# Feed-forward input products in a seven-product form, and modulation products in 512-wide pieces

## The chip, the cores and the metric

One core of a Trainium2 chip runs the whole program. The metric is device time in microseconds, the median of a few executions.

## The reference, cut to what matters

A two-layer backbone works on 640 tokens (128 context tokens, 512 latent ones) of width 1024, in float32. Each layer is a feed-forward half step, a mixer, and a second feed-forward half step:

```python
def swiglu(h, w_in, w_out):
    a, b = jnp.split(h @ w_in, 2, axis=-1)      # w_in: 1024 x 5632
    return (jax.nn.silu(a) * b) @ w_out         # w_out: 2816 x 1024

def ffn_half_step(x, mods, g, w_in, w_out):
    shift, scale, gate = mods
    return x + 0.5 * gate * swiglu(rmsnorm(x, g) * (1.0 + scale) + shift, w_in, w_out)
```

The mixers are a pooling and short-convolution mixer in layer 0 and an attention mixer in layer 1. Each layer has nine modulation vectors per condition (one condition for the context, one for the latent tokens): `silu(cond) @ mod_w + mod_b`, of which `mod_w` is 1024 x 9216 for each layer.

## The kernel before

**Layout.** Activations lie transposed: 128 features on the partitions, tokens along the free axis. The 640 tokens are two halves of 320 (`HALVES`). A matrix product in float32 is made of three products of rounded parts: each operand is split into a rounded part (`hi`, type fp32r) and the rest (`lo`), and `mm3` (lines 110 to 115) issues hi·hi, hi·lo and lo·hi. `split_w` (lines 95 to 101) makes the parts of a weight tile of 128 x 1024: ScalarE writes `whi`, VectorE subtracts and writes `wlo`; each has five buffers.

**A feed-forward stage** (`ffn`, four of them) goes over 22 pairs `j`: a 128-wide column block of the gate side and the matching one of the value side. `load_pair` loads two weight tiles of 512 KB and splits them. `pair_half` multiplies both by the normalised activations `h_hi`, `h_lo` of one token half (8 blocks of the contraction, three matmuls each), and `pair_tail` makes silu of the one times the other and splits the result into `ghi`, `glo`. So a pair is 2 sides x 2 halves x 8 blocks x 3 = 96 matmuls of 320 columns. After 4, 8, 12 and 17 pairs a group of pairs is complete; `out_group` multiplies it by its w_out tiles one pair later (8 output blocks x 2 halves x group size x 3 matmuls: 192 for a group of four) and `add_x` adds each block to `x` with the gate, in one VectorE instruction for the second half and two for the first. The last group goes through `out_last`, which computes the norm sums and the next stage's `h` on the way. Pairs 0 and 1 are done together, from weights that were fetched in the stage before; `me.second()` writes the second half of `h` while the first half multiplies.

**Modulation.** `gemv(l, m, q)` is one quarter of one modulation vector: two 512 KB loads (`mraw`, two buffers of its own), then on VectorE, for each of two conditions, one `tensor_scalar` and seven `scalar_tensor_tensor` of 256 columns, a transpose and a reduction of 512 columns. `todo` is the list of quarters; `step()` takes one after each pair and `drain()` takes what is left at the stage's end. The four feed-forward stages are given 6, 4, 5 and 1 vectors.

**Order of the work.** Engines run their instructions in order. The order is written by a scheduler at compile time: each instruction has the priority of its place in the program text, and on each engine the earliest instruction that the scheduler's own timeline holds to be ready goes next. The buffers of one tag are handed out to the instructions in the same way. TensorE's instructions follow the text almost exactly; VectorE's and ScalarE's may run ahead of it as far as buffers allow. All loads are issued from SyncE's queue.

## Time and profile before

| | |
|---|---|
| time, median of 3 runs | 2528.28 us |
| the three runs | 2528.28, 2528.24, 2536.61 us |
| span of the profiled execution | 2535.1 us |
| TensorE busy | 2485.0 us, 98% |
| VectorE busy | 1604.7 us, 63% |
| ScalarE busy | 731.5 us, 29% |
| granted TensorE clock, mean | 0.987 |

The profile is of one execution, from its first to its last instruction. Its own time is not listed apart from the three; the span fits the third, 2536.61 us, which leaves 1.5 us around it. Busy time of TensorE counts pipelined matmuls, so it says that matmuls followed each other, not how fast.

### The profile page before, as it was taken

The numbers are of one execution on the slowest core, as the hardware profiler recorded it, in microseconds if no ns is written. First come the engines' busy times: TensorE is split into PE (matmuls) and PEld (weight loads), VectorE is DVE, ScalarE is ACT, GpSimd is POOL, SyncE is SP. The second block draws the span as 40 slices with busy tenths as digits, with TensorE's granted clock in tenths as the row PEclk, the third lists the DMA queues.
The fourth block names the chain that finished last, engine by engine and source line by source line (L and its number), as shares of the span: only waits on it lengthen the run. The fifth ranks groups of instructions, "written<-read, shape, count | busy, mean of one in ns | idle before, by whom it ended". The sixth has DMA issues, their size and how long they took to land.

```text
span 2535.1 us, 40930 instructions
## 1 busy us (share of the span) xinstructions
PE 2485.0 (98%) x16594; PEld 2417.9 (95%) x16594; DVE 1604.7 (63%) x3520; ACT 731.5 (29%) x1339; POOL 155.5 (6%) x156
## 2 busy tenths in 40 slices
PE   6999999999999999999999999999999999999998
PEld 3999999999999999999999999999988799999998
DVE  6999993376599974337999933444447787333334
ACT  3322221243242222223222221344334442221222
POOL 2000000031110000002000000211001110000001
PEclk8999999999999999999999999999999899999999
DMA  7444442232144432222544412122111023222221
GB/s 262 134 159 149 167 142 75 67 94 82 59 134 150 165 118 84 72 70 84 167 158 151 150 67 76 67 86 80 49 64 36 17 93 116 75 75 75 75 76 42
DMA packets 81691, 257.44 MB, mean 102 GB/s; under 512 B 12896, under 2 KB 18656, under 8 KB 81504
## 3 DMA queue, kind: packets, MB, share of 16 engines
q1 hardware_dynamic: 81504, 254.84, 30.3%
q8 instruction: 130, 2.13, 0.4%
q14 instruction: 57, 0.47, 0.1%
HBM read 251.13 MB, written 3.67 MB: 101 GB/s over the span
## 4 chain that ended last, share of the span: by engine, by line
PE 94%; DVE 4%; DMA 1%; ACT 1%; issue 0%; SPq 0%; DVEq 0%; ACTq 0%
PE mm L113 25%; PE mm L114 25%; PE mm L115 25%; PE atb L723 2%; PE mmb L113 2%; PE mmb L114 2%; PE mmb L115 2%; PE sd L789 1%; PE m L114 1%; PE m L113 1%; PE m L115 1%; PE atb L717 1%; PE mmb L622 1%; PE mmb L623 1%; PE mmb L624 1%; PE sn L743 1%
## 5 line engine op out<-in xcount | busy, mean ns | idle before, releaser
L114 PE MATMUL mm<-h_lo,whi 128*128 128x320 f32 x2944 | 906.0, 308 | 1.7 <-DVE h_lo L233 1.7
L115 PE MATMUL mm<-h_hi,wlo 128*128 128x320 f32 x2944 | 906.5, 308 | 0.0
L113 PE MATMUL mm<-h_hi,whi 128*128 128x320 f32 x2944 | 901.1, 309 | 2.2 <-ACT h_hi L231 1.8
L99 ACT CAST whi<-raw 128x1024 fp32r<-128x1024 f32 x320 | 335.4, 1050 | 859.6 <-PE mm L114 762.6
L114 PEld LDWEIGHTS mm<-h_lo,whi 128*128 128x128 f32 x2944 | 553.0, 188 | 2.4 <-DVE h_lo L233 2.0
L113 PEld LDWEIGHTS mm<-h_hi,whi 128*128 128x128 f32 x2944 | 551.2, 188 | 3.6 <-ACT h_hi L231 2.0
L115 PEld LDWEIGHTS mm<-h_hi,wlo 128*128 128x128 f32 x2944 | 553.1, 188 | 0.0
L100 DVE TENSOR_TENSOR wlo<-raw,whi 128x1024 fp32r<-128x1024 f32 x302 | 371.9, 1232 | 215.5 <-ACT whi L99 214.6
L113 PE MATMUL mm<-ghi,whi 128*128 128x320 f32 x1408 | 436.4, 310 | 0.0
L115 PE MATMUL mm<-ghi,wlo 128*128 128x320 f32 x1408 | 435.8, 309 | 0.0
L114 PE MATMUL mm<-glo,whi 128*128 128x320 f32 x1408 | 435.4, 309 | 0.0
L143 DVE SCALAR_TENSOR_TENSOR gacc<-mraw,sc,gacc 128x256 f32<-128x256 f32 x896 | 383.5, 479 | 0.2
L239 DVE SCALAR_TENSOR_TENSOR x<-mm,gate,x 128x128 f32<-128x128 f32 (+2 forms) x480 | 195.2, 435 | 175.3 <-PE mm L115 174.5
L115 PEld LDWEIGHTS mm<-ghi,wlo 128*128 128x128 f32 x1408 | 264.7, 188 | 0.0
L113 PEld LDWEIGHTS mm<-ghi,whi 128*128 128x128 f32 x1408 | 264.7, 188 | 0.0
L114 PEld LDWEIGHTS mm<-glo,whi 128*128 128x128 f32 x1408 | 264.7, 188 | 0.0
L348 DVE TENSOR_TENSOR g<-silu,mm 128x320 f32<-128x320 f32 x168 | 81.8, 487 | 268.8 <-PE mm L115 267.2
L193 POOL TENSOR_TENSOR acc<-acc,sq 128x320 f32<-128x320 f32 x84 | 79.5, 946 | 1973.2 <-ACT sq L188 1966.1
L350 ACT CAST ghi<-g 128x320 fp32r<-128x320 f32 x176 | 80.4, 457 | 285.2 <-DVE g L348 284.9
L346 ACT ACTIVATE silu<-mm 128x320 f32<-128x320 f32 x168 | 72.8, 433 | 198.0 <-PE mm L115 197.8
L351 DVE TENSOR_TENSOR glo<-g,ghi 128x320 fp32r<-128x320 f32 x176 | 85.2, 484 | 21.6 <-ACT ghi L350 21.6
L188 ACT ACTIVATE sq<-x 128x320 f32<-128x320 f32 x98 | 45.6, 469 | 118.4 <-DVE x L239 91.2
(201 smaller groups left out, 2504.0 us busy)
## 6 DMA issues: line engine op xcount, KB each, us to landing
raw<-w_in SPq DMA_DIRECT2D x176, 512.0 KB
mraw<-mod_w SPq DMA_DIRECT2D x128, 512.0 KB
raw<-w_out SPq DMA_DIRECT2D x88, 512.0 KB
m<-mod_w SPq DMA_DIRECT2D x32, 256.0 KB
raw<-even_w SPq DMA_DIRECT2D x16, 512.0 KB
raw<-mix_w SPq DMA_DIRECT2D x16, 512.0 KB
raw<-odd_qk SPq DMA_DIRECT2D x16, 512.0 KB
raw<-odd_v SPq DMA_DIRECT2D x8, 512.0 KB
```

Of the source, the lines that this page charges most:

```text
L99: act.copy(hi, src)
L100: eng.tensor_tensor(lo, src, hi, ALU.subtract)
L113: pe.matmul(out, wh, xh, start=start, stop=False)
L114: pe.matmul(out, wh, xl, start=False, stop=False)
L115: pe.matmul(out, wl, xh, start=False, stop=stop)
L143: dve.scalar_tensor_tensor(out=acc[:, c, :], in0=w[k], scalar=sc[:, k, c:c + 1], in1=acc[:, c, :], op0=ALU.mult, op1=ALU.add)
L193: pool.tensor_tensor(acc, acc, s, ALU.add)
L239: dve.scalar_tensor_tensor(out=x[:, k, a:b], in0=ps[:, a - a0:b - a0], scalar=gate[:, c, k:k + 1], in1=x[:, k, a:b], op0=ALU.mult, op1=ALU ...
L346: act.activation(s, pa, AF.Silu)
L348: dve.tensor_tensor(g, s, pb, ALU.mult)
L350: act.copy(ghi[:, a:b], g)
L351: dve.tensor_tensor(glo[:, a:b], g, ghi[:, a:b], ALU.subtract)
```

## The change

**Seven products.** From pair 3 on (`NPLAIN = 3`) a pair is computed in Strassen's form. The 2 x 2 blocks are: halves of the tokens, halves of the contraction (blocks 0 to 3 and 4 to 7), and gate or value side. Seven products of four blocks each (7 x 4 x 3 = 84 matmuls) replace eight (96). `strassen_w` makes four sums of half weight tiles on VectorE and splits three whole tiles and one half tile where before two whole ones were split. Sums of `h` are made once per stage: `sums` after pairs 0 and 1, `sums7` after pair 2, into `q_hi`, `q_lo` and over the second half of `h_hi`, `h_lo`. For the next stages `h_chunk` writes the second half of an unsplit copy of `h` with one more ScalarE instruction per block. Partial results leave PSUM by four ScalarE copies and four VectorE sums per pair, and two accumulators are added to again after they were copied.

**Modulation.** A piece is now one 512 KB load and four VectorE instructions of 512 columns; four pieces make half a vector and end with two transposes and two reductions. The loads take their buffers from the weights' own ring (`raw`, five buffers where the weights had three). After pair 2 and each later pair `step` takes at least three pieces. One vector of layer 0 moves from the first feed-forward stage to the mixer behind it, so the stages now have 5, 1 (in the mixer), 4, 5 and 1 vectors, of eight pieces each.

**Buffers.** `ghi` and `glo` go from ten buffers to seven, the small tiles share one ring of eight.

```diff
+NPLAIN, GBUFS = 3, 7
...
-            w = wpool.tile([128, 1024], F32, tag="raw", bufs=3, name="raw")
+            w = wpool.tile([128, 1024], F32, tag="raw", bufs=5, name="raw")
...
+        def strassen_w(src_a, src_b):
+            ra, rb = load_w(src_a), load_w(src_b)
+            tt = scope[0].tile([128, 1024], F32, tag="tt", bufs=1, name="tt")
+            dve.tensor_tensor(tt[:, 512:1024], ra[:, 0:512], rb[:, 0:512], ALU.add)
+            x0 = split_w(ra)
+            dve.tensor_tensor(tt[:, 0:512], tt[:, 512:1024], rb[:, 512:1024], ALU.add)
+            dve.tensor_tensor(rb[:, 0:512], rb[:, 0:512], rb[:, 512:1024], ALU.add)
+            dve.tensor_tensor(ra[:, 0:512], tt[:, 0:512], ra[:, 512:1024], ALU.add)
+            x1 = split_w(tt)
+            x2 = split_w(rb)
+            hi = scope[0].tile([128, 512], F32R, tag="whi4", bufs=1, name="whi4")
+            lo = scope[0].tile([128, 512], F32R, tag="wlo4", bufs=1, name="wlo4")
+            act.copy(hi, ra[:, 0:512])
+            dve.tensor_tensor(lo, ra[:, 0:512], hi, ALU.subtract)
+            return [(t[0][:, o:o + 512], t[1][:, o:o + 512]) for t in (x0, x1, x2) for o in (0, 512)] + [(hi, lo)]
...
-        def gemv(l, m, q):
-            w = load_mod(A["mod_w"][l, m, q])
-            acc = scope[0].tile([128, 2, 256], F32, tag="gacc", bufs=1, name="gacc")
...
+        def gemv(l, m, q, i):
+            w = wpool.tile([128, 1024], F32, tag="raw", bufs=5, name="mraw")
+            sp.dma_start(out=w, in_=A["mod_w"][l, m, q, i])
+            if i == 0:
+                accs[0] = scope[0].tile([128, 2, 512], F32, tag="gacc", bufs=1, name="gacc")
+            acc = accs[0]
+            for j in range(2):
+                k, wk = 2 * i + j, w[:, j * 512:(j + 1) * 512]
                 for c in range(2):
...
+            for c in range(2):
+                at = scope[0].tile([128, 16, 32], F32, tag="gaccT", bufs=1, name="gaccT")
+                dve.transpose(at.rearrange("p b i -> p (b i)"), acc[:, c, :])
+                dve.tensor_reduce(part[:, c, 16 * q:16 * q + 16], at, axis=AX.X, op=ALU.add)
...
+        def step(n=2):
+            for _ in range(min(n, len(todo))):
+                gemv(*todo.popleft())
...
+                if whole is not None:
+                    act.activation(whole[:, a:b], t[:, a - a0:b - a0], AF.Identity, bias=sh[:, c, k:k + 1])
...
+                def sums(hs):
+                    n = NT if me.y is None else HT
+                    for k in range(8):
+                        dve.tensor_tensor(hs[k][:, 0:n], h_hi[:, k, 0:n], h_lo[:, k, 0:n], ALU.add)
+                    for k in range(4):
+                        (a11, a21), (a12, a22) = [(t[:, 0:HT], t[:, HT:NT]) for t in (hs[k], hs[k + 4])]
+                        dve.tensor_tensor(a22, a21, a22, ALU.subtract)
+                        dve.tensor_tensor(a21, a11, a21, ALU.subtract)
+                        dve.tensor_tensor(a11, a22, a11, ALU.subtract)
+                        dve.tensor_tensor(a12, a12, a11, ALU.add)
+                        for d, src in ((slice(0, 2), hs[k + 4].rearrange("p (a n) -> p a n", a=2)),
+                                       (slice(2, 3), a11.unsqueeze(1))):
+                            act.copy(q_hi[:, k, d, :], src)
+                            dve.tensor_tensor(q_lo[:, k, d, :], src, q_hi[:, k, d, :], ALU.subtract)
+
+                def sums7(hs):
+                    for k in range(4):
+                        act.copy(h_hi[:, k, HT:NT], hs[k][:, HT:NT])
+                        dve.tensor_tensor(h_lo[:, k, HT:NT], hs[k][:, HT:NT], h_hi[:, k, HT:NT], ALU.subtract)
...
+                def strassen_pair(j):
+                    b11, b21, t2, t1, t3, b22, t4 = strassen_w(w_in[2 * j], w_in[2 * j + 1])
+                    new_g(j)
+
+                    def prod(out, w, xs, first=True):
+                        for k in range(4):
+                            mm3(out, w, k, xs[k][0], xs[k][1], first and k == 0, k == 3, True)
+
+                    a, b = mmb([128, HT], "pa"), atb([128, HT], "pb")
+                    prod(a, b11, hs_op(0, 0))
+                    c11 = t320("t")
+                    act.copy(c11, a)
+                    prod(b, b21, hs_op(4, 0))
+                    dve.tensor_tensor(c11, b, c11, ALU.add)
+                    act.activation(c11, c11, AF.Silu)
+                    prod(a, t2, q_op(2), False)
+                    c12 = t320("t")
+                    act.copy(c12, a)
+                    ec = sb2("pe")
+                    e, c = ec[:, 0:HT], ec[:, 512:512 + HT]
+                    prod(e, t1, q_op(1))
+                    c22 = t320("t")
+                    act.copy(c22, e)
+                    prod(a, t3, hs_op(0, 1), False)
+                    c21 = t320("t")
+                    act.copy(c21, a)
+                    dve.tensor_tensor(c22, c22, a, ALU.subtract)
+                    prod(e, b22, q_op(0), False)
+                    dve.tensor_tensor(c12, e, c12, ALU.subtract)
+                    dve.tensor_tensor(c11, c11, c12, ALU.mult)
+                    g_split(j, c11, 0)
+                    prod(c, t4, hs_op(4, 1))
+                    dve.tensor_tensor(c21, c, c21, ALU.add)
+                    act.activation(c21, c21, AF.Silu)
+                    dve.tensor_tensor(c21, c21, c22, ALU.mult)
+                    g_split(j, c21, 1)
...
-                        step()
                         j = 2
...
+                    else:
+                        strassen_pair(j)
+                        j += 1
+                    if j == 2:
+                        sums(hs)
+                    if j == NPLAIN:
+                        sums7(hs)
+                    if j >= NPLAIN:
+                        step(max(3, -(-len(todo) // (NPAIR - j + 1))))
                     if pend is not None:
...
-                drain()
+                step(len(todo))
...
-            return [(l, m, q) for m in ms for q in range(4)]
+            return [(l, m, q, i) for m in ms for q in range(2) for i in range(4)]
...
-        todo.extend(pieces(0, 2, 3, 4, 5, 6, 7))
+        todo.extend(pieces(0, 2, 3, 4, 5, 6))
         ffn(0, FFN1, n_ffn[0][0], n_even, start)
+        todo.extend(pieces(0, 7))
         even_mixer(n_even, n_ffn[0][1])
```

## Rows read from the trace of the kernel before

**Rows 1.** The page: busy time of each engine, its share, instructions.

```profile
PE 2485.0 (98%) x16594; PEld 2417.9 (95%) x16594; DVE 1604.7 (63%) x3520; ACT 731.5 (29%) x1339; POOL 155.5 (6%) x156
```

**Rows 2.** The page: the chain that ended last, by engine.

```profile
PE 94%; DVE 4%; DMA 1%; ACT 1%; issue 0%; SPq 0%; DVEq 0%; ACTq 0%
```

**Rows 3.** Windows: four feed-forward stages, and a stretch inside the first.

```profile
core 0: us, PE busy (x) PEld busy (x) DVE busy (x) ACT busy (x) POOL busy (x), PEclk, DMA share, GB/s
...
200.00:400.00 200.00, 200.00 (x1367) 200.00 (x1366) 176.73 (x387) 45.54 (x68) 0.00 (x0) 1.00 0.45 147
...
72.00:540.00 468.00, 468.00 (x3203) 467.93 (x3204) 361.48 (x800) 120.89 (x196) 16.84 (x29) 1.00 0.39 128
710.00:1172.00 462.00, 460.19 (x3137) 459.93 (x3136) 297.97 (x634) 113.43 (x179) 9.37 (x10) 1.00 0.33 110
1195.00:1660.00 465.00, 464.94 (x3181) 464.60 (x3180) 332.33 (x716) 119.85 (x192) 16.77 (x16) 1.00 0.36 119
2053.00:2515.00 462.00, 462.00 (x3157) 462.00 (x3157) 209.47 (x406) 115.96 (x186) 8.74 (x10) 1.00 0.23 76
```

**Rows 4.** Groups by form, VectorE, 72 to 200 us: count, busy, mean, idle before.

```profile
L143 DVE SCALAR_TENSOR_TENSOR gacc<-mraw,sc,gacc 128x256 f32<-128x256 f32 x138 | 59.1, 477 | 0.1
L100 DVE TENSOR_TENSOR wlo<-raw,whi 128x1024 fp32r<-128x1024 f32 x20 | 24.3, 1216 | 1.6 <-ACT whi L99 1.5
L351 DVE TENSOR_TENSOR glo<-g,ghi 128x320 fp32r<-128x320 f32 x15 | 7.2, 482 | 0.0
L348 DVE TENSOR_TENSOR g<-silu,mm 128x320 f32<-128x320 f32 x14 | 6.8, 487 | 3.9 <-PE mm L115 3.1 <-issue 0.5
L146 DVE STREAM_TRANSPOSE gaccT<-gacc 128x512 f32<-128x512 f32 x9 | 6.4, 708 | 0.2
L150 DVE TENSOR_REDUCE part<-gaccT 128x16 f32<-128x512 f32 x9 | 6.1, 679 | 0.1
L140 DVE TENSOR_SCALAR gacc<-mraw,sc 128x256 f32<-128x256 f32 x20 | 6.1, 346 | 0.0
L239 DVE SCALAR_TENSOR_TENSOR x<-mm,gate,x 128x320 f32<-128x320 f32 x8 | 4.4, 547 | 1.3 <-PE mm L115 1.3
L239 DVE SCALAR_TENSOR_TENSOR x<-mm,gate,x 128x192 f32<-128x192 f32 x8 | 3.3, 406 | 0.0
L239 DVE SCALAR_TENSOR_TENSOR x<-mm,gate,x 128x128 f32<-128x128 f32 x8 | 2.8, 345 | 0.4 <-PE mm L115 0.4
```

**Rows 5.** Windows: the same stretch as rows 4.

```profile
72.00:200.00 128.00, 128.00 (x875) 128.00 (x876) 120.11 (x270) 34.92 (x55) 0.00 (x0) 1.00 0.47 156
```

**Rows 6.** Groups by form, VectorE, whole run: forms near the new ones.

```profile
L233 DVE SCALAR_TENSOR_TENSOR h_lo<-hn,mod,h_hi 128x320 fp32r<-128x320 f32 x48 | 25.5, 563 | 0.9 <-ACT h_hi L231 0.9
...
L544 DVE SCALAR_TENSOR_TENSOR cv<-z,small,cv 128x512 f32<-128x512 f32 x8 | 8.0, 998 | 0.1
...
L318 DVE TENSOR_TENSOR yn<-yn,nps 128x640 f32<-128x640 f32 x4 | 3.0, 815 | 1.7 <-PE nps L216 1.7
...
L475 DVE TENSOR_TENSOR d<-win,inv 128x512 f32<-128x512 f32 x4 | 2.7, 680 | 0.0
...
L541 DVE TENSOR_SCALAR cv<-z,small 128x512 f32<-128x512 f32 x4 | 1.9, 486 | 0.1
```

**Rows 7.** Groups by form, ScalarE, whole run.

```profile
L99 ACT CAST whi<-raw 128x1024 fp32r<-128x1024 f32 x320 | 335.4, 1050 | 859.6 <-PE mm L114 762.6 <-issue 46.3 <-PE m L114 29.2
...
L346 ACT ACTIVATE silu<-mm 128x320 f32<-128x320 f32 x168 | 72.8, 433 | 198.0 <-PE mm L115 197.8
...
L639 ACT COPY k<-mmb 128x320 f32<-128x320 f32 x12 | 5.1, 421 | 3.5 <-PE mmb L115 3.5
```

**Rows 8.** Windows: the layer-0 mixer, and a gap of TensorE in it.

```profile
556.00:566.00 10.00, 6.93 (x46) 6.41 (x45) 10.00 (x11) 5.89 (x10) 3.69 (x5) 1.00 0.53 152
566.00:590.00 24.00, 24.00 (x155) 23.99 (x154) 22.57 (x40) 7.63 (x13) 8.92 (x8) 0.93 0.40 131
545.00:691.00 146.00, 142.66 (x960) 141.91 (x959) 90.57 (x160) 43.56 (x68) 24.20 (x21) 0.99 0.23 76
```

More of the change, by code (lines that the diff above doesn't have):

```diff
@@ L335, in load_pair @@
                 def load_pair(j):
[L336 to L337 removed]
+                    return [split_w(load_w(w_in[2 * j + i])) for i in range(2)]
                 def new_g(j):
@@ L360, in ffn, with make_gate @@
+                def make_gate():
+                    gate = tmp.tile([128, 2, 8], F32, tag="gate", bufs=2, name="gate")
+                    for c in range(2):
+                        dve.tensor_scalar(gate[:, c, :], modt[l][:, 3 * which + 2, c, :], 0.5, None, op0=ALU.mult)
+                    return gate
                 gate = None
@@ L370, in ffn @@
                             if half:
-                                if not SECOND:
-                                    me.second()
                                 p = [t[:, o:o + HT] for t in (sb2("m2"), sb2("m2")) for o in (0, 512)]
-                            else:
-                                p = [bank([128, HT]) for _ in range(4)]
-                            if half:
                                 units_k(zip_l(p[0:2], w0), half)
@@ L379, in ffn @@
                             else:
+                                p = [bank([128, HT]) for _ in range(4)]
                                 units_k(zip_l(p[0:3], (w0[0], w0[1], w1[0])), half)
-                            if SECOND and not half:
-                                with tc.high_priority(P_H):
-                                    me.second()
+                                me.second()
                             pair_tail(0, p[0], p[1], half)
```

115 lines of the change are left out of this document (53 added, 62 removed).

## The prediction

> **What bounds the kernel now.** I read the page first: TensorE is busy 98% of the span [rows 1], and the chain that ended last is TensorE for 94% [rows 2]. A busy share could hide matmuls that start late, so the next view is the windows. Inside the first feed-forward stage 1367 matmuls start in 200 us, one every 0.1465 us, with the clock granted in full, and in the four stages TensorE has next to no idle time [rows 3]. So a matmul of 320 columns that goes away in these stages gives back 0.1465 us, as long as nothing else becomes the pace. VectorE is what could: in the same four windows it is busy 361, 298, 332 and 209 us of some 465, 77% in the first and 45% in the last [rows 3]. The difference is modulation, of which the stages do 24, 16, 20 and 4 quarters. The groups by form of the first stage's beginning show what a VectorE without reserve looks like: 120 of 128 us busy, and half of it `gacc` [rows 4, 5].
>
> **How much VectorE does in a microsecond.** The ten groups shown add up to 134 us by count times mean, and the 21 other instructions, put at 0.3 us each, make it 140 us in 128 us of time [rows 4, 5]. Durations overlap, and little waiting is left. So I divide durations by 140/128 = 1.09 to get time on a full VectorE. The bounds: without the 8 us of idle the divisor is 140/120 = 1.17; if nothing overlapped it is 1.0. The Trainium skill ("VectorE: DVE Perf Modes", section "The DRAIN you can't avoid") says that the next operation does not start until the pipe is empty, which would make it 1.0, and the sum below +139 instead of +36. The trace does not agree: 140 us of durations fit into 128.
>
> **TensorE, removed.** 19 pairs in each of four stages, 96 - 84 = 12 matmuls each: 912 x 0.1465 = 133.6 us, 33.4 per stage. A pair becomes 12.3 us (was 14.1), three plain pairs are 42.2, a group of four w_out tiles stays 28.1.
>
> **VectorE, added.** A plain pair has two `wlo` and four operations of 320 columns: 2 x 1.216 + 4 x 0.485 = 4.4 us [rows 4]. A seven-product pair has four sums of 512 (0.68, the nearest row with the same shape [rows 6]), three `wlo` of 1024 and one of 512 (0.68), and eight operations of 320: 2.7 + 3.65 + 0.7 + 3.9 = 10.9 us, which is 10.0 on a full VectorE. A modulation piece has operations of 512 columns that the stages don't show. `scalar_tensor_tensor` goes from 0.345 at 128 to 0.547 at 320 columns [rows 4], a line that gives 0.75 at 512; the only row of that width is 0.998 [rows 6], in the mixer; I take the line, since its rows come from the stages themselves, and the other row is the upper bound. With `tensor_scalar` at 0.486 [rows 6] half a vector is 2 x 0.486 + 14 x 0.75 + 2 x 0.708 + 2 x 0.679 = 14.2 us, so a piece is 3.56, or 3.26 on a full VectorE. The old quarter was 2 x 0.346 + 14 x 0.477 + 0.708 + 0.679 = 8.8, so a vector falls from 35 to 28 us. A w_out group of four costs 4 x 1.216 + 8 x (0.547 + 0.406 + 0.345) = 15.2, or 14.0 [rows 4]. The sums of `h` are 16 operations of 320, eight of 320 or 640 (0.815 [rows 6]), and four pairs of 640 and 320: 17 us, 19 in the first stage, plus 2 behind pair 2.
>
> **What sets the end.** The list of pieces is not spread over a stage: three follow each pair from pair 2 on, and they stand in the text ahead of the next pair's `strassen_w`. On a VectorE that is behind, the earlier instruction goes first, so the next weights wait behind three pieces. They also wait in SyncE's queue: pieces and weights share five buffers, so a weight load is issued only when a piece has freed one. In a stretch with pieces, four pairs and a w_out group cost VectorE 4 x (10.0 + 3 x 3.26) + 14.0 = 93 us, and TensorE 4 x 12.3 + 28.1 = 77 us, where the old form took 84. So VectorE is the pace there, and the stretch is slower than before. Behind it TensorE is the pace and the gain is whole. A lead cannot be carried into the stretch, since only about one pair of weights fits into the five `whi`.
>
> Stage by stage, the stall that is to be set against 33.4 us:
> - First stage. Before pair 3, VectorE has six tails (5.8), one plain pair's `wlo` (2.4), the sums (19), three pieces (10.7) and pair 3's weights (7.0): 45 us, 41 on a full VectorE, against 42.2 on TensorE; no stall. The 40 pieces last to pair 15: VectorE 13 x 10.0 + 37 x 3.26 + 3 x 14.0 = 293, TensorE 13 x 12.3 + 3 x 28.1 = 244. Stall 48.
> - Second (32 pieces, to pair 12). The second half of `h` comes on top, eight blocks at 0.55 and 0.563 [rows 6], so the start is 5 us late; then 10 x 10.0 + 29 x 3.26 + 28 = 222 against 179. Stall 48.
> - Third (40 pieces): 5 + 48 = 53.
> - Fourth (8 pieces): 5, and two pairs with five pieces, 36 against 25 us. Stall 17.
> - The layer-0 mixer gets eight pieces, 26 us of VectorE, half of them among the pool sums, where TensorE already waits 3 of 10 us for VectorE [rows 8]. I take 4; bounds 0 and 13.
>
> Sum: 48 + 48 + 53 + 17 + 4 = 170 us of stall against 133.6 saved, +36. With the divisor 1.17 the stalls are 100 and the sum is -34; with 1.0 they are 273 and it is +139 (`gacc` at 0.998 instead of 0.75 would add 94 by itself). The profiled execution has 2535.1 us of span and probably 2536.6 of time, 8.3 over the median; I take these 8 us off both: 2528 + 36 = **2565 us**, own range 2494 to 2667.
>
> **Edits put at nothing.** ScalarE goes from 2 x 1.05 + 4 x 0.44 = 3.9 to 3.5 x 1.05 + 8 x 0.44 = 7.2 us a pair [rows 7], under TensorE's 12.3. Transfers: 20 weight and piece loads and four of w_out in 93 us are 12.6 MB, 135 GB/s, where these stretches move 147 to 156 now [rows 3, 5]; if a load came late, it would be one weight tile per pair. Seven `ghi`: a group is read out one pair after it is complete, while only the next pair's tile is being written; if they were short, a tail would wait, and TensorE only a pair later.
>
> **The rivals.**
> 1. The pieces give way (chance 0.29). If VectorE's order lets the weights go first, only a stage's total counts. The first stage: 361 - 24 x 8.8/1.09 + 40 x 3.26 + 19 x (10.9 - 4.4)/1.09 + 20 = 431 us, against TensorE's 468 - 33 = 435; the third 431 against 432; the second 404 and the fourth 334. It just fits, and what is left are the late starts and the mixer, 19 us: 2528 - 134 + 19 = 2413. For it: the present `gacc` already runs ahead of its place without holding up TensorE. Against it: in the text pieces come first. This is the faster side, and it decides as soon as four pairs cost VectorE under 84 us.
> 2. The clock falls (0.13). After a gap of 3.1 us in the mixer the granted clock is 0.93 over the next 24 us, so 3.4 us of it ran at 1.2 GHz [rows 8], a loss of 1.7 us. 38 pairs lie in stretches with pieces; if each loses 1.7 us beyond my sum, that is 65 us: 2630, and more where the clock stays low. Against it: slow matmuls run while TensorE would wait anyway. The Trainium skill ("TensorE: Matmul & The Clock Gate", section "HAM oscillation — how this bites in real kernels") says that a wait in every step makes each step start at the low clock; by that rule all 38 would pay.
> 3. ScalarE's copies hold up TensorE (0.10). An accumulator that was copied is added to again one product, 1.76 us, later. One cast ahead of the copy, 1.05 + 0.42 [rows 7], is hidden; two are not, and cost 0.8 us. At one such case in each of the 38 pairs outside the stretches: 30 us on top, 2595.
>
> **Chances.** The forecast has 0.48, of which 0.09 falls under -0.5%, 0.11 within it and 0.28 over it. With the rivals: faster 0.38, same 0.11, slower 0.51; half a percent, 12.6 us, is about what a measurement of this kernel can tell from no change. The range reaches down to the first rival and up into the second: 2405 to 2640.
>
> **What would show it.** Right: in windows over pairs 3 to 15 of the first and third stage VectorE is over 90% busy, TensorE waits some 5 us in each pair for `whi` and `wlo`, and behind the last piece the matmuls close up again; the fourth stage is shorter than before by some 15 us. The 512-wide `gacc` shows 0.75 us, a sum 0.68. Wrong: TensorE over 97% busy in the first stage while VectorE is near 93% (rival 1), a granted clock under 0.8 (rival 2), TensorE's waits put down to ScalarE's copies (rival 3), or a piece that costs another time than 3.3 us; 0.3 us on each of 116 pieces outside TensorE's cover is 35 us in the sum.

## The result, and the profile after

The changed kernel takes 2607.93 us (median of 4 runs, 2603.21 to 2611.43), beside 2531.78 us for the kernel before in the same job: ratio 1.0293, 95% interval 1.0267 to 1.0319. The forecast was 2565.

Of the page after, busy time and the chain, which answer to [rows 1, 2]:

```profile
PE 2417.3 (93%) x15682; PEld 2326.1 (89%) x15682; DVE 2027.3 (78%) x3912; ACT 993.7 (38%) x1867; POOL 151.4 (6%) x156
...
PE 73%; DVE 22%; issue 2%; DMA 2%; ACT 1%; SPq 0%; DVEq 0%; ACTq 0%
```

TensorE has 912 matmuls fewer and the kernel is still slower: TensorE was 98% busy and 94% of the chain, now 93% and 73%, and VectorE has 22% of the chain. Where the time lies is seen by stage. Windows of the kernel after; the columns are those of [rows 3]. First stage, layer-0 mixer, second stage, third stage, attention mixer, fourth stage:

```profile
53.00:559.00 506.00, 463.61 (x2994) 452.57 (x2995) 442.10 (x810) 185.54 (x324) 13.70 (x12) 0.96 0.34 109
559.00:765.00 206.00, 187.21 (x1220) 184.69 (x1219) 147.13 (x282) 62.05 (x110) 33.28 (x45) 0.95 0.28 90
765.00:1241.00 476.00, 448.11 (x2982) 442.96 (x2981) 410.89 (x752) 186.56 (x328) 15.24 (x14) 0.97 0.35 109
1241.00:1737.00 496.00, 457.26 (x2988) 449.71 (x2988) 435.91 (x795) 187.87 (x329) 15.49 (x14) 0.96 0.35 113
1737.00:2133.00 396.00, 386.91 (x2390) 338.93 (x2389) 219.31 (x572) 167.21 (x418) 42.41 (x39) 0.97 0.18 55
2133.00:2592.00 459.00, 441.80 (x2980) 439.75 (x2980) 337.53 (x616) 188.68 (x332) 15.13 (x16) 0.98 0.25 78
```

The same parts in the kernels compared below, each from its first matmul to the first of the next part (us, from the traces; the names are those of the experiments):

| part | before | after | no pieces | plain | spread | norm first | combined | attention | form alone |
|---|---|---|---|---|---|---|---|---|---|
| opening | 44.8 | 53.2 | 52.8 | 53.5 | 52.1 | 49.1 | 57.4 | 57.1 | 59.6 |
| stage 1 | 479.4 | 506.0 | 450.9 | 476.0 | 478.6 | 505.4 | 476.3 | 475.6 | 494.7 |
| layer-0 mixer | 182.3 | 205.7 | 186.2 | 205.4 | 205.5 | 202.1 | 185.4 | 185.4 | 206.9 |
| stage 2 | 473.4 | 476.6 | 445.9 | 486.6 | 464.2 | 480.6 | 464.1 | 463.7 | 492.1 |
| stage 3 | 470.0 | 495.8 | 444.8 | 485.5 | 462.0 | 491.3 | 459.7 | 447.7 | 488.8 |
| attention mixer | 398.9 | 395.5 | 389.8 | 388.5 | 389.0 | 391.4 | 394.9 | 406.4 | 398.8 |
| stage 4 | 472.0 | 458.7 | 447.9 | 487.8 | 459.1 | 464.1 | 460.9 | 445.1 | 468.2 |
| end | 14.1 | 14.1 | 14.1 | 14.1 | 14.0 | 14.1 | 14.1 | 14.1 | 14.0 |

No edit up to "attention" is aimed at the attention mixer, and its 388 to 399 us go with the clock: without the time lost to the low clock it takes 383 to 387 us in each of these kernels. So differences of some 10 us in this part say nothing about an edit.

Inside the stages there are two kinds of place where time is lost: the stretches with pieces, and the beginnings (pairs 0 to 2). Windows of the kernel after. First fence: the stretch with pieces in stage 1 (pairs 3 to 15), in stage 2 (pairs 3 to 12) and in stage 3 (pairs 3 to 15), and what lies behind the last piece in stage 1. Second fence: the beginning of stage 2, and the two pairs with pieces in stage 4:

```profile
104.00:402.00 298.00, 261.66 (x1655) 255.63 (x1655) 287.21 (x512) 103.51 (x176) 0.00 (x0) 0.94 0.40 128
827.00:1067.00 240.00, 226.43 (x1491) 222.87 (x1490) 232.65 (x418) 85.05 (x141) 0.00 (x0) 0.97 0.42 131
1305.00:1582.00 277.00, 256.38 (x1658) 251.46 (x1657) 263.99 (x466) 96.36 (x162) 0.00 (x0) 0.96 0.41 132
...
402.00:510.00 108.00, 104.20 (x688) 103.00 (x687) 78.42 (x129) 43.08 (x69) 0.00 (x0) 0.97 0.30 94
```

```profile
765.00:827.00 62.00, 47.68 (x305) 46.31 (x304) 61.85 (x131) 27.95 (x58) 1.51 (x2) 0.86 0.27 85
...
2199.00:2253.00 54.00, 53.38 (x365) 53.15 (x364) 44.83 (x85) 18.58 (x31) 0.00 (x0) 1.00 0.32 105
```

The stretch of stage 1 has 1655 matmuls, 242.5 us at 0.1465, and takes 298 with VectorE 96% busy; that of stage 3 takes 277 for 243. Behind the last piece 688 matmuls, 101 us' worth, take 108, so TensorE nearly has the pace again. The 55 us of stage 1's stretch are not spread evenly over its pairs: 29 are lost in the first 66 us, 5 in the next 126 and 21 in the last 106, though VectorE is 95% busy or more in all three:

```profile
104.00:170.00 66.00, 46.88 (x252) 43.72 (x252) 65.87 (x123) 23.80 (x41) 0.00 (x0) 0.82 0.38 127
170.00:296.00 126.00, 121.52 (x824) 120.47 (x823) 120.60 (x218) 42.91 (x73) 0.00 (x0) 1.00 0.40 126
296.00:402.00 106.00, 93.26 (x581) 91.44 (x582) 100.74 (x173) 36.80 (x63) 0.00 (x0) 0.94 0.41 132
```

The beginnings are what I hadn't looked for. In 62 us the beginning of stage 2 does 305 matmuls, 44.7 us' worth; VectorE is busy all the time, and the clock is at 0.86, so some 17 us of it at 1.2 GHz. The same beginning before:

```profile
706.00:755.00 49.00, 47.03 (x313) 46.51 (x312) 45.34 (x108) 19.73 (x41) 1.76 (x2) 0.97 0.40 132
```

What TensorE waited for, over the whole run after (engine, tile and line, what it waited for: us, times, longest):

```profile
PE nps L227 <- DVE dg L224: 32.1, 5, 9.0
PE pa L123 <- DVE wlo L100: 16.5, 11, 3.6
PE mm L121 <- ACT whi L99: 16.2, 7, 3.8
PE pa L121 <- ACT whi L99: 11.5, 9, 2.3
...
PE gps L169 <- DVE part L166: 8.5, 4, 5.7
...
PE pa L121 <- ACT t L425: 2.6, 5, 0.5
```

`whi` and `wlo` were forecast. The first row was not: `nps` is the small matmul that spreads the second half's norm, and it waits for `dg`, the last of twelve dependent steps, eleven of them on three elements (`rinv`, lines 222 to 224). The timeline of VectorE there (start, duration, instruction):

```profile
774.27 0.15 DVE L222 TENSOR_SCALAR rv<-nps 128x3 f32<-128x3 f32 x1
...
776.20 0.15 DVE L210 SCALAR_TENSOR_TENSOR rt<-rt,rv 128x3 f32<-128x3 f32 x1
776.27 0.88 DVE L154 TENSOR_SCALAR gacc<-mraw,sc 128x512 f32<-128x512 f32 x2
777.06 0.16 DVE L211 SCALAR_TENSOR_TENSOR ry<-rt,ry 128x3 f32<-128x3 f32 x1
777.13 1.41 DVE L156 SCALAR_TENSOR_TENSOR gacc<-mraw,sc,gacc 128x512 f32<-128x512 f32 x2
778.46 0.16 DVE L209 TENSOR_TENSOR rt<-ry 128x3 f32<-128x3 f32 x1
778.53 1.41 DVE L156 SCALAR_TENSOR_TENSOR gacc<-mraw,sc,gacc 128x512 f32<-128x512 f32 x2
...
788.80 0.56 DVE L224 TENSOR_TENSOR dg<-ident,ry 128x384 f32<-128x384 f32 x1
```

Between two steps of the norm stand two operations of a piece, or sums of `strassen_w`. From `rv` at 774.27 to `dg` at 788.80 it is 14.5 us. In the kernel before the same chain took 2.8, most of its steps 0.2 us apart; its first and last step there, and then TensorE's wait in the kernel after, from 780.9 to 789.4:

```profile
715.94 0.15 DVE L211 TENSOR_SCALAR rv<-nps 128x3 f32<-128x3 f32 x1
...
718.76 0.56 DVE L213 TENSOR_TENSOR dg<-ident,ry 128x384 f32<-128x384 f32 x1
```

```profile
789.41 1.54 PE L227 MATMUL nps<-dg,ones 128*128 128x128 f32 x6 [8.55 <-DVE dg L224]
```

### The profile page after: what moved, and what is told of

The parts are those of the page before. It is cut to its first block, busy times and chain, and to the rows that moved or that the text cites. A ratio compares the mean times of both kernels' runs of the same rounds, so it can differ in the third digit from the quotient of the medians.

```text
span 2605.6 us, 39946 instructions
## 1 busy us (share of the span) xinstructions
PE 2417.3 (93%) x15682; PEld 2326.1 (89%) x15682; DVE 2027.3 (78%) x3912; ACT 993.7 (38%) x1867; POOL 151.4 (6%) x156
## 4 chain that ended last, share of the span: by engine, by line
PE 73%; DVE 22%; issue 2%; DMA 2%; ACT 1%; SPq 0%; DVEq 0%; ACTq 0%
PE mm L121 10%; PE mm L122 10%; PE mm L123 10%; DVE gacc L156 5%; PE pa L121 4%; PE pa L123 4%; PE pa L122 4%; PE pe L121 4%; PE pe L123 4%; PE pe L122 4%; DVE wlo L100 3%; PE mmb L121 2%; PE mmb L122 2%; PE atb L813 2%; PE mmb L123 2%
## 5 line engine op out<-in xcount | busy, mean ns | idle before, releaser
L99 ACT CAST whi<-raw 128x1024 fp32r<-128x1024 f32 x320 | 334.4, 1049 | 438.2 <-PE mm L122 185.4
L156 DVE SCALAR_TENSOR_TENSOR gacc<-mraw,sc,gacc 128x512 f32<-128x512 f32 x448 | 326.5, 760 | 0.2
L121 PE MATMUL pe<-q_hi,whi 128*128 128x320 f32 x608 | 193.8, 319 | 4.7 <-ACT whi L99 3.2
L121 PE MATMUL pa<-h_hi,whi 128*128 128x320 f32 x608 | 188.8, 311 | 10.0 <-ACT whi L99 7.4
L123 PE MATMUL pa<-h_hi,wlo 128*128 128x320 f32 x608 | 188.1, 310 | 5.5 <-DVE wlo L100 5.5
L123 PE MATMUL pe<-q_hi,wlo 128*128 128x320 f32 x608 | 191.6, 316 | 1.6 <-DVE wlo L100 1.6
L122 PE MATMUL pe<-q_lo,whi 128*128 128x320 f32 x608 | 192.0, 316 | 1.0 <-DVE q_lo L394 1.0
L122 PE MATMUL pa<-h_lo,whi 128*128 128x320 f32 x608 | 187.8, 309 | 0.0
L122 PE MATMUL mm<-h_lo,whi 128*128 128x320 f32 x512 | 160.0, 315 | 4.8 <-DVE h_lo L244 4.8
L121 PE MATMUL mm<-h_hi,whi 128*128 128x320 f32 x512 | 154.4, 316 | 7.5 <-DVE modA L186 3.8
L123 PE MATMUL mm<-h_hi,wlo 128*128 128x320 f32 x512 | 159.1, 313 | 0.0
```

The lines of the kernel that those rows point to most:

```text
L99: act.copy(hi, src)
L121: pe.matmul(out, wh, xh, start=start, stop=False, skip_group_check=skip)
L122: pe.matmul(out, wh, xl, start=False, stop=False, skip_group_check=skip)
L123: pe.matmul(out, wl, xh, start=False, stop=stop, skip_group_check=skip)
L156: dve.scalar_tensor_tensor(out=acc[:, c, :], in0=wk, scalar=sc[:, k, c:c + 1], in1=acc[:, c, :], op0=ALU.mult, op1=ALU.add)
```

## The experiments

All ran beside the kernel before, whose median was 2528.4 to 2533.6 us in these jobs. A ratio is against that kernel in the same job, with its 95% interval behind it. Diffs are against the changed kernel unless said otherwise.

**1. No pieces.** In `gemv`:

```diff
-            for j in range(2):
-                k, wk = 2 * i + j, w[:, j * 512:(j + 1) * 512]
...
+            dve.tensor_scalar(acc[:, 0, 0:2], w[:, 0:2], sc[:, 0, 0:1], None, op0=ALU.mult)
             if i < 3:
                 return
...
-                dve.transpose(at.rearrange("p b i -> p (b i)"), acc[:, c, :])
-                dve.tensor_reduce(part[:, c, 16 * q:16 * q + 16], at, axis=AX.X, op=ALU.add)
+            dve.memset(part[:, :, 16 * q:16 * q + 16], 0.0)
```

> Leaves out the modulation sums: each piece is still loaded, but VectorE makes one product of two columns instead of four of 512, and the transposes and reductions are a memset. Four theories. Pace: VectorE sets the pace where pieces stand ahead of the next weights. Chain: pieces that are loaded before a stage begins stand between the steps of the norm's chain of small VectorE operations, and in the mixer between the pool sums. Clock: each gap is followed by time at 1.2 GHz. Form: the seven products themselves hold up TensorE, by their copies and PSUM sums. Pace, chain and clock all say that the stages close up: 2532 - 134 + 8 for the late kernel start + some 10 = 2416 us. Form says that most of the time stays, above 2500 us.

2434.16 us, ratio 0.9615 (0.9598 to 0.9633), 18 above the 2416 that three of the four theories gave. The form on TensorE is not slow; in the changed kernel the pieces' work on VectorE costs 174 us. Stage 2 and its beginning without pieces:

```profile
690.00:1135.00 445.00, 439.54 (x2979) 438.14 (x2979) 323.12 (x631) 188.55 (x328) 15.17 (x14) 0.99 0.37 117
```

```profile
690.00:743.00 53.00, 47.54 (x302) 46.35 (x302) 49.96 (x118) 28.02 (x59) 1.47 (x2) 0.90 0.39 129
```

From their first matmul to that of pair 3, the beginnings of stages 2 to 4 last 53.9, 52.6 and 56.6 us here, 48.3, 44.6 and 47.6 before, 62.6, 63.5 and 66.5 after. So of the 52.1 us that the three beginnings grew by, 29.5 go with the pieces' work; the other 22.6 are there without it, and I put them down to the sums of `h` and the first four-sum weights.

**2. Plain.** The change without the seven products: all pairs by `load_pair` and `pair_half`, no sums of `h`.

```diff
-                    elif j < NPLAIN:
+                    elif j < NPAIR:
```

> The change without the seven products: all 22 pairs in the old form, no sums of h; wide pieces, three per pair, the shared ring, the moved vector and the buffer counts stay. Pace: four plain pairs with three pieces each and a group cost VectorE 4 x (4.4 + 10.7) / 1.09 + 14 = 69 us against 84 on TensorE, no stall in the stretches: 2532 + 8 for the start = 2540 us, if nothing else is lost. Chain: the stage starts and the mixer lose as before, some 12 us in three stages and 20 in the mixer: 2595 us. Form: 2532 us.

2599.8 us, 1.0266 (1.0248 to 1.0283), as the chain theory has it and not the pace theory. The modulation part alone is nearly as slow as the whole change. Stage 1 is no longer than before; stages 2 to 4 are 13 to 16 us longer, the mixer 23, the opening 9. `nps` waits 25.9 us for `dg`. That is not the pace in the stretches: VectorE is 60% and 65% busy in stages 2 and 3 (291 and 314 us of 486 and 485). All that the three stages lose lies in their beginnings, 61.4, 60.1 and 63.3 us long. Stage 2, its beginning and the rest of it:

```profile
735.00:796.00 61.00, 48.40 (x305) 47.02 (x304) 55.92 (x112) 18.98 (x38) 1.57 (x2) 0.86 0.37 121
796.00:1221.00 425.00, 425.00 (x2906) 425.00 (x2905) 235.04 (x415) 101.33 (x156) 13.58 (x12) 1.00 0.32 105
```

The norm is stretched to 12.9 us here (12.6 and 13.4 ahead of stages 3 and 4), on a VectorE that has work for 55% of the rest of the stage. So 13 to 16 us a stage are lost at the stretched chain and right behind it, in a beginning with VectorE 92% busy, without a shortage of VectorE time in the stage as a whole.

**3. Own ring.** The pieces' loads get buffers of their own as before.

```diff
-            w = wpool.tile([128, 1024], F32, tag="raw", bufs=5, name="raw")
+            w = wpool.tile([128, 1024], F32, tag="raw", bufs=3, name="raw")
...
-            w = wpool.tile([128, 1024], F32, tag="raw", bufs=5, name="mraw")
+            w = scope[0].tile([128, 1024], F32, tag="mraw", bufs=scope[2], name="mraw")
```

(`scope[2]` is 2 in the stages and 1 in the mixers.)

> The modulation pieces get two buffers of their own in each stage's pool again (one in the mixer), and the weights three; all else as changed. A piece can then not be loaded before its stage begins. Chain: the three stage starts get back some 12 us each, the mixer up to 20, the kernel's start 8: 2545 us. Pace: the stretches still have three pieces ahead of each pair's weights: 2608 us, no change.

2587.09 us, 1.0218 (1.02 to 1.0236), and not for the reason expected: stage 2 takes 476 us as after, and its norm still stretches over 12.7 us, though the first piece's load is issued only 3 us ahead of it. Of the 21 us, 12 are in stage 1, 4 in stage 3, 2 in the layer-0 mixer and 8 in the attention mixer, which has no pieces and differs by the clock alone; the opening is 7 us longer. The shared ring is not what breaks up the norm ahead of stages 2 to 4. Ahead of the mixer it is whole again (2.2 us instead of 13.4), and the mixer gains only 2 us by it.

**4. Spread.** The same pieces, in the same places of the text, but no longer three behind each pair:

```diff
-                        step(max(3, -(-len(todo) // (NPAIR - j + 1))))
+                        step(max(3 if j < 6 else 1, -(-len(todo) // (NPAIR - j + 1))))
```

> From pair 5 on the pieces are spread evenly over the pairs that are left (two per pair in the stages with 40, one or two with 32) instead of three per pair until they are used up; all else as changed. Pace: four pairs and a group then cost VectorE 4 x (10.0 + 2 x 3.26) + 14 = 80 us against 77, so the first and third stage get back some 25 us each and the second 15: 2545 us. Chain: 2608 us, no change.

2528.5 us (10 runs), 0.9987 (0.9972 to 1.0002): 79 us less than the changed kernel, more than the pace theory asked for, with the same VectorE work. Stages 1 and 3 win 27 and 34, stage 2 12, and the attention mixer 6 by its clock; beginnings, layer-0 mixer and opening stay as they were. Stage 3 of this run, TensorE and VectorE 441 and 432 of 461 us:

```profile
1201.00:1662.00 461.00, 441.22 (x2980) 437.72 (x2979) 431.93 (x791) 186.24 (x326) 15.20 (x14) 0.98 0.39 122
```

**5. Norm first.** One order more on VectorE: `last[0]` is the `dg` of the norm begun last, and what is traced in such a block is queued behind it.

```diff
-                gemv(*todo.popleft())
+                with tc.issue_after(last[0]):
+                    gemv(*todo.popleft())
...
-                        sums(hs)
+                        with tc.issue_after(last[0]):
+                            sums(hs)
```

(and so `load_pair` and `strassen_w`.)

> The changed kernel with one order added on VectorE: pair 2's and the seven-product pairs' weight sums and splits, the token sums of the second halves and the modulation products are queued behind the last step (dg) of the norm that was begun before them. No instruction is added or taken away. Chain theory (the second half's norm, twelve dependent steps on 3 elements, is stretched from 2.8 to 14.5 us by long operations that stand between its steps, TensorE waits 9 us for dg and then runs at half clock): the chain takes 3 us again, TensorE's wait for dg falls from 9 to about 2 us, the beginnings of the second, third and fourth stage (62.6, 63.5 and 66.5 us to the first seven-product pair) come down by about 12 us each, 2570 us in all. Work theory (the same VectorE work has to be done before pair 2 and pair 3 can start, so what is put behind the norm is late afterwards): the wait for dg goes, one for whi or wlo takes its place, 2600 to 2615 us.

2601.09 us, 1.027 (1.0236 to 1.0305), inside the work theory's range: the chain is stretched by what stands between its steps, but mending it alone gives little. The norm before stage 2, from its first steps to `dg`:

```profile
765.72 0.15 DVE L228 TENSOR_SCALAR rv<-nps 128x3 f32<-128x3 f32 x1
765.90 0.17 DVE L212 TENSOR_SCALAR ry<-rv 128x3 int32<-128x3 int32 x1
...
767.67 0.16 DVE L216 SCALAR_TENSOR_TENSOR ry<-rt,ry 128x3 f32<-128x3 f32 x1
767.87 0.56 DVE L230 TENSOR_TENSOR dg<-ident,ry 128x384 f32<-128x384 f32 x1
```

2.1 us instead of 14.5, and the beginnings of stages 2 to 4 take 52.2, 52.1 and 56.5 us instead of 62.6, 63.5 and 66.5: 32 us won. They are paid back at once: the rest of the three stages takes 37 us more, and the 7 us of the whole run come from the opening and the mixers. Windows of this run, the beginning of stage 2 and the 66 us behind it:

```profile
757.00:809.00 52.00, 47.20 (x307) 46.13 (x306) 51.62 (x113) 26.57 (x56) 1.16 (x2) 0.93 0.23 71
809.00:875.00 66.00, 51.31 (x317) 49.18 (x316) 64.12 (x116) 18.53 (x31) 0.00 (x0) 0.90 0.42 137
```

After the change, without this edit, the 66 us behind the beginning hold 399 matmuls; here 317. TensorE now stands elsewhere, first of all at the small matmul that folds a finished modulation vector:

```profile
PE gps L173 <- DVE part L170: 27.3, 8, 9.7
PE pa L127 <- DVE wlo L100: 21.8, 15, 3.7
PE pa L125 <- ACT whi L99: 20.6, 12, 3.0
```

The work theory holds: VectorE is 99% busy in the beginning and 97% in the 66 us behind it, and whatever is put first, the rest is late.

**6. Vector back.** The moved vector's eight pieces go back into stage 1, none are in the mixer (in the text, `pieces(0, 7)` moves from the one list to the other).

> The changed kernel with the eight pieces of the one modulation vector that the change moved into the layer-0 mixer back in the first feed-forward stage; the mixer has none. Place theory (the pieces, not the longer pool sums or the buffers, make the mixer longer): mixer from 205.7 to about 185 us, the first stage longer by what 8 pieces cost there in VectorE-full pairs, 8/3 pairs by some 5 us = 13; 2600 us in all. Rival (the mixer is long for another reason, such as its starting chain): mixer stays at 205, first stage +13, 2621 us.

2594.77 us, 1.0242 (1.0215 to 1.027): the mixer falls from 205.7 to 185.4 us, stage 1 rises from 506.0 to 517.8, as the place theory says. The mixer in this run, with TensorE 181 of 186 us:

```profile
571.00:757.00 186.00, 180.84 (x1219) 179.86 (x1218) 123.46 (x237) 62.72 (x110) 34.27 (x45) 0.98 0.25 77
```

**7. Opening's loads.** The loads of pieces, and of weights behind the first four, are issued behind the last load `m` of the opening.

```diff
-            sp.dma_start(out=w, in_=A["mod_w"][l, m, q, i])
+            with tc.issue_after(lastm[0]):
+                sp.dma_start(out=w, in_=A["mod_w"][l, m, q, i])
```

> The changed kernel with the loads of the modulation pieces and of the weights after the first four units issued behind the last load of the opening vectors (m). Queue theory (the shared ring of five lets these loads go ahead of the opening vectors, and the first h matmul waits for those): first h matmul at about 46 instead of 53.2 us, 2601 us. Rival (the opening is bound by VectorE, or by the buffers of m, of which the change leaves 14 instead of 16): 53 as before, 2608 us.

2589.68 us, 1.0222 (1.0195 to 1.025), but the queue theory fell: the first `h` matmul starts at 57.5 us, later than the 53.2 after. The gain is in stage 1 (490.6): its beginning takes 43.6 instead of 50.6 us, and its first piece starts at 68.0 instead of 78.6, which would leave less for the crowded pairs behind. Why the opening grew by 8 us stays open; in the trace after, the first `hn` of the opening starts at 47.7 us, behind the second half's norm, where before it started at 40.1. It is longer than the 44.8 us before in every kernel of the table, without the pieces' products (52.8), without the seven products (53.5) and with the old modulation in its own ring (59.6). What all of these keep, among other edits, is the new buffer counts, which no run takes back.

**8. Combined.** Spread, norm first, vector back, opening's loads.

> The three edits of this call together with the even spread of the pieces over the pairs. If they lie in different places and add up: 2608 less 79 (spread, measured) less 36 (chain), less 7 to 20 (vector) and 7 (start), that is 2465 to 2480 us, faster than before by some 2 per cent. Rival (VectorE's total work in a stage is the bound, so that what is gained at one place is paid at another): 2510 to 2530 us, no better than the spread alone.

2514.01 us, 0.9917 (0.9888 to 0.9947), 14 us less than the spread alone: the rival's range, not the sum. Against the spread alone the layer-0 mixer gives 20 us; stages 1 to 3 stay within 3 us although stage 1 has eight pieces more. The beginnings of stages 2 to 4 are 11, 12 and 14 us shorter than with the spread alone, and the three stages as wholes within 3 us: paid back here too.

**9. Late fold.** Norm first, and the fold of a finished vector one step later; for the gate, behind the first two units of the w_out group.

```diff
+                folds.append((l, m, part))
...
         def step(n=2):
+            flush()
...
+                    held = [out_mm(ws, k, gs, acts, half, bankf) for half in range(2)]
+                    gate = gate()
```

(`flush` issues the waiting folds and their additions; `gate` calls it too, and `out_mm` is a unit's matmuls without its addition to `x`.)

> The changed kernel with the norm's order of the earlier run and one edit more: TensorE's small matmul that folds a finished modulation vector (gps) is issued a pair later, and the one that the gate needs behind the first two units of the w_out group. After the norm's order alone TensorE stood 5.7, 7.5 and 9.7 us before this matmul in stages 1, 2 and 4, until VectorE had the vector's last sum. Place theory (what the norm's order gave was lost again at this one matmul): those waits shrink by what is issued ahead (two units, 3.5 us, and what follows on half clock), stages 2 and 4 shorter by 5 to 10 us each, 2580 us. Work theory (VectorE is behind by then, and TensorE stands at the next weights instead): whi or wlo takes its place, 2596 to 2604 us.

2589.67 us, 1.0226 (1.0193 to 1.0259), between the two theories. Against experiment 5 stage 1 wins 8 us and stage 4 wins 3, stage 3 loses 3. In stage 4 TensorE stands at the fold for 10.4 us where it was 9.7, for a `part` that comes later too. The work theory fits this better.

**10. Attention.** The combined kernel with the late fold, and with layer 1's last three vectors in the attention mixer instead of stages 3 and 4:

```diff
-        todo.extend(pieces(1, 3, 4, 5, 6, 7))
+        todo.extend(pieces(1, 3, 4, 5))
...
+        todo.extend(pieces(1, 6, 7, 8))
         odd_mixer(n_odd, n_ffn[1][1])
-        todo.extend(pieces(1, 8))
```

(with `step(3)` behind six of its projections and the rest ahead of a w_out group.)

> The earlier combination (even spread, norm's order, moved vector back in the first stage, loads behind the opening vectors) with the late fold, and with the pieces of layer 1's last three vectors in the attention mixer, where VectorE has work for 243 of 395 us, instead of the third and fourth stage. Place theory (a stage is long by what its own pieces take of VectorE): third stage from 460 to about 452 us with 24 pieces instead of 48 less 40 added elsewhere, fourth from 461 to 449 with none, attention mixer longer by up to 10; 2495 us. Rival (24 pieces stretch the attention mixer's chains of small steps as they stretch the norm): attention mixer +20 or more, 2515 or more, no better than the earlier combination.

2497.12 us, 0.9863 (0.9835 to 0.9891), where the place theory put it, and the fastest that keeps all the work. Stage 3, attention mixer, stage 4:

```profile
1182.00:1630.00 448.00, 441.00 (x2985) 438.02 (x2984) 386.60 (x706) 187.99 (x330) 15.65 (x15) 0.99 0.33 106
1630.00:2036.00 406.00, 389.80 (x2391) 341.38 (x2389) 294.45 (x705) 167.16 (x415) 41.46 (x39) 0.96 0.27 85
2036.00:2481.00 445.00, 440.71 (x2975) 439.55 (x2976) 313.08 (x569) 189.15 (x332) 13.86 (x16) 0.99 0.22 71
```

Stages 3 and 4 come within 3 us of what they take without any piece (444.8, 447.9): with 24 pieces spread over a stage VectorE has room. Against the combined kernel the two stages win 28 us and the mixer gives back 11, some 5 of these by its clock.

**11. Before without pieces.** The kernel before, the products of its quarters replaced by touches.

```diff
-            for c in range(2):
-                dve.tensor_scalar(acc[:, c, :], w[0], sc[:, 0, c:c + 1], None, op0=ALU.mult)
...
+            for k in range(0, 8, 2):
+                dve.tensor_scalar(acc[:, 0, 0:2], w[k][:, 0:2], sc[:, 0, 0:1], None, op0=ALU.mult)
```

> The kernel before with the products of the modulation pieces left out (each loaded block touched by one two-column operation, the vectors' sums set to zero), its loads kept: what the pieces cost there. Hidden theory (in the kernel before TensorE sets the pace with VectorE at 80 per cent, so the pieces cost next to nothing): 2505 to 2530 us, and against the changed kernel without pieces (2434) the seven-product form alone is worth 70 to 95 us. Rival (the pieces already cost before, in stalls that close up, and the change only makes them dearer): below 2490 us.

2562.23 us, 1.0122 (1.0085 to 1.0159): slower than the kernel with the products, which neither theory foresaw, so I take no cost of pieces from it. VectorE waits for the loads where the touches now stand:

```profile
DVE gacc L140 <- DMA mraw<-mod_w: 168.3, 106, 4.0
```

and TensorE stands 5.4, 6.2 and 5.4 us at the first w_out group of stages 1 to 3. VectorE is busy 1197.7 us here and 1604.7 in [rows 1]; leaving these 407 us out won nothing, which fits products that were hidden before, but with the new waits it doesn't show it.

**12. Form alone.** The seven products with the modulation as before: 256 wide, a quarter at a step, own ring, three weight buffers, the vector in stage 1.

```diff
-                        step(max(3, -(-len(todo) // (NPAIR - j + 1))))
+                    if j == 2:
+                        step()
+                    step()
```

> The other part alone: the seven-product form of the changed kernel with the modulation products of the kernel before (256 wide, a quarter of a vector at a step, a step a pair and two after pair 1, the moved vector in the first stage, own ring of two loads for them, three buffers for weights). A quarter is 16 products of some 0.48 us, so a vector takes 64 x 0.48 = 31 us of durations where the wide form takes 32 x 0.76 = 24, 19 vectors 120 us more in all. Order theory (the loss of the changed kernel comes from the order of the pieces, three a pair from the first seven-product pair on; one quarter a pair is an even spread): about the time of the spread run, 2515 to 2545 us, although VectorE has more to do. Amount theory (VectorE's sum in a stage decides): first and third stage each longer by the 38 us that six vectors take more, 2580 to 2610 us. If the seven-product form itself were slow on TensorE, above 2608.

2618.56 us, 1.0336 (1.03 to 1.0372): above the amount theory's range, and far from the order theory. A quarter a pair is even, but VectorE is 96%, 87% and 93% busy in stages 1 to 3 all the same, and the fold, with VectorE behind, becomes the largest wait of TensorE:

```profile
PE gps L169 <- DVE part L166: 70.2, 9, 13.5
```

An even order helped only as far as the stage's sum fits: the narrow products don't fit beside the seven-product form; the wide ones, spread and placed as in experiment 10, nearly do. This run changes the width, the ring and the buffers together, and narrow products with the late fold were not run, so how much of it is the width alone isn't shown.

## Why the prediction came out as it did

**Right: what sets the end.** VectorE took over the pace behind pair 2, in the order that the text gives, and the pieces went ahead of the weights. Experiment 1 (174 us for the pieces) and experiment 4 (79 us for their order alone) show it. The forecast sign of some 5 us of waits in each pair came out weaker and uneven: TensorE is idle for 36 of the 298 us in stage 1's stretch, and the other 19 us of its loss are slow matmuls. TensorE's saving is there: without pieces stages 1 to 4 take 24 to 29 us less than before, against 33.4 forecast, and in stages 2 to 4 the dearer beginnings (6 to 9 us) are about the rest. This sets a kernel without pieces against one with them, and experiment 11 gives no control for that; that the pieces cost next to nothing before rests on [rows 3], where TensorE has next to no idle time in the stages.

**Right: the prices.** Groups by form in pairs 3 to 15 of stage 1, after:

```profile
L156 DVE SCALAR_TENSOR_TENSOR gacc<-mraw,sc,gacc 128x512 f32<-128x512 f32 x126 | 91.3, 758 | 0.1
L100 DVE TENSOR_TENSOR wlo<-raw,whi 128x1024 fp32r<-128x1024 f32 x37 | 45.3, 1230 | 1.0 <-ACT whi L99 1.0
...
L109 DVE TENSOR_TENSOR raw<-raw 128x512 f32<-128x512 f32 x12 | 8.4, 702 | 0.0
```

0.758 us for the wide `gacc` (forecast 0.75 from the line through 128 and 320 columns), 0.702 for a sum (0.68). In stage 1's stretch VectorE was to need 293 us, and the stretch took 298. One reading is to be set right: the section of the Trainium skill that the prediction holds against the overlap of durations ("VectorE: DVE Perf Modes", section "The DRAIN you can't avoid") goes on to say that a next operation that is not held starts earlier, so the overlap in the traces does not speak against the page.

**Mis-sized: the terms of the sum.** The spans differ by 70.5 us (2605.6 and 2535.1), forecast +36.

| term | forecast | measured | from |
|---|---|---|---|
| stretches with pieces, four stages | 48 + 43 + 48 + 12 = 151 | 55 + 22 + 34 + 1 = 112 | windows, less 0.1465 a matmul |
| beginnings of stages 2 to 4 | 5 + 5 + 5 = 15 | 14 + 19 + 19 = 52 | 62.6, 63.5, 66.5 against 48.3, 44.6, 47.6 |
| layer-0 mixer | 4 | 23 | 205.7 against 182.3 |
| opening | 0 | 8 | 53.2 against 44.8 |

The first line came out lower by 39 and the other three higher by 64; the attention mixer is 3 shorter; and 12 us are left without a line of their own, 7 of them behind the last piece of stage 1 (the 108 us for 101 us' worth): 36 - 39 + 64 - 3 + 12 = 70.

The first two lines together are 166 forecast and 164 measured, so what the stages lose came out rightly as a sum and wrongly divided. That the sum fits owes something to luck, since the forecast knew of no exchange between the two. The step that failed is the layer-0 mixer's term, "I take 4; bounds 0 and 13": it measured 23, outside both bounds, and experiment 6 shows that its eight pieces make 20 of them. Beside it the opening, a term put at nothing without a reason, measured 8; its cause stays open. These two are 27 of the 34 us by which the sum fell short.

I read the mixer and the start that was to be "5 us late" (14 to 19 measured) as the same error. I counted what VectorE has to do, as busy time, and not what it does to a chain of small dependent steps: where VectorE always has something ready, the order puts it between two of them. For the starts the timeline and experiment 5 show this. In the mixer TensorE waits 4.0 us for `dg` and 5.3 for `dhi` of the pool sums; in experiment 5 the mixer's norm takes 2.1 us instead of 13.4, the mixer still 202.1, and its longest wait is now 7.2 us for `yb` of the convolution. So the norm alone is not it; how much each of the mixer's chains costs isn't shown.

In the changed kernel the stretched norm is not an extra that a better order gives back (experiment 5: 32 us won at the beginnings, 7 in all). It is one place among several at which the same surplus of VectorE work is paid: at `dg`, at `part`, at `whi` and `wlo`. Experiment 2 shows the other case: with VectorE idle for 45% of the rest of a stage, the beginnings with the stretched chain lose 13 to 16 us all the same, and whether the norm's order would give that back was not run. What gives time back here is less VectorE work in the crowded stretch: pieces later in the stage (79 us, of which 6 are the attention mixer's clock), out of the layer-0 mixer (20, of which stage 1 takes 12 back in experiment 6), into the attention mixer (17 net, with the late fold).

**The second stage** was forecast +15 and came out +3: its stretch lost 22 us, not 43, and that hid the 14 at its beginning. Experiment 5 moved such a loss from the one to the other, so only the sum of a stage can be held against the forecast.

**The 8 us.** The forecast stands on the median of the runs shown, 8 us under the profiled execution. The profiled execution after took 2607.4 us beside a median of 2607.9, so there the reduction has no counterpart: of the 43 us between 2565 and 2608, 8 are this and the rest the terms.

**The rivals.** Pieces that give way (2413): not so, as experiment 4 shows by what their order costs. ScalarE's copies (2595): TensorE waits for them, but for 3.7 us in the whole run (the largest of these waits is the row `t L425` in the result), so not to the amount of the rival.

The falling clock (2630) is there, mostly as a follower. Mean granted clock went from 1.00 to 0.94 in the stretch of stage 1, which is 18 us lost over 13 pairs, 1.4 a pair where the rival said 1.7; but the stretch took only 5 us more than the 293 I gave it, and VectorE was 96% busy in it, so I take it that slow matmuls cost little there. The Trainium skill ("TensorE: Matmul & The Clock Gate", section "HAM oscillation — how this bites in real kernels") describes a kernel in which a wait in every step makes each step start at the low clock. These rows agree in part: the clock is 0.82 and 0.94 at the two ends of the stretch and 1.00 in the 126 us between them. The beginning of stage 2 lost 62 x 0.14 = 9 us to the clock, half of what it lost in all, right behind the wait for `dg`; VectorE was full there too, so whether this half would have been lost anyway isn't shown.

Over the whole run the time lost to the clock rose from 33 to 104 us (mean clock 0.987 and 0.960), as much as the kernel grew by. No run takes the clock's part out by itself. It is not all of the cause: the spread kernel has the same matmuls and loses 76 us to it (0.970), 28 less than the changed kernel, where it is 79 us faster.

## What to carry to other kernels

When one engine's work is moved to a second that has idle time, add up the second by stretch and not by its mean, and by what the order of the text puts together there; the same pieces spread over the stage were worth 79 us here. A full engine also stretches the short dependent chains that pass through it, at stage borders and norms (14.5 us instead of 2.8 here), so these must be priced in steps times the length of what can stand between two, not in busy time. Where that engine has no room, mending one of the places where its surplus shows (a norm, a fold) only moved it here: first move work to where the engine is idle.

## What the runs showed of the hardware

The recorded durations of VectorE's operations overlap. In the timeline of the result two wide `gacc` of 0.75 us take 1.41 us together, and a step of three elements with a duration of 0.15 us is followed after 0.07 us by an instruction that doesn't depend on it (776.20 to 776.27). In the timeline of experiment 5 a dependent step follows after 0.2 us.
